# Spreading attention bias rows two heads at a time in a one-core encoder step

## The chip, the cores and the metric

The kernel runs on one core of one Trainium2 chip. A core has five engines with their own instruction queues, each served in order: TensorE (PE in the profile, with its weight loads listed apart as PEld) multiplies, VectorE (DVE) and ScalarE (ACT) work element by element and read the accumulators in PSUM, GpSimd (POOL) works on SBUF, and SyncE (SP) issues most of the transfers. Transfers are issued from the queues of SP, ACT and POOL, and the profile shows 16 DMA engines that carry them. The metric is the device time of one execution of the whole program in microseconds (us); lower is better.

## The reference

One layer of a streaming encoder runs for two groups of requests that share the weights: 2048 prompt rows and 128 sample rows (8 requests of 16 rows), 1024 wide. In float32:

```python
h = rms_norm(x, norm_g[0])
z = h @ w_in                      # q, k, v of attention (8 heads x 64); q, k, v, o of the mLSTM (4 x 128); gates
att = chunk-band attention(z)     # own 64-row chunk + 8 before it; + rel_bias(rel_table), clipped at 256
att = rms_norm(att, g_att)
hb  = mlstm_sequence(z)           # matrix memory with input and forget gates, running-max stabiliser
mix = concat(att, normed hb * sigmoid(o)) @ w_out
x   = x + rms_norm(mix, norm_g[1])
x   = x + rms_norm(conv_ffn(rms_norm(x, norm_g[2])), norm_g[3])
```

The sample rows attend to a cache of 512 keys and values per request and head and to their own 16 rows, and start the mLSTM from a given state. The outputs are the rows, the new keys and values, the memory's state and the convolution's tail. The bias of a score depends on the distance of query and key alone, so one row of 767 numbers per head holds all of it.

## The kernel before

All matrix products of the projections and of the feed-forward part are done in three passes: each operand is split into a high part (a cast to fp32r) and a low part (the difference), and `mm3` (L105 to L107) adds high x high, high x low and low x high in PSUM.

The program has two phases. In the first, the normed rows are transposed and multiplied by `w_in` in 14 groups of columns for each half of the rows (`GROUPS`: `va0`, `qk0`, `qk1`, `va1`, and so on to `vo3`). `group_T` and `group_rows` compute a group: each output tile is accumulated in one of two PSUM buffers (`ps_mm`), copied by ScalarE to one of two SBUF buffers (`st`), and stored to DRAM through ScalarE's queue (`qTd`, `kTd`, `vd`, `qkbd`, `vobd`). Group `va0` also holds the 8 gate columns, which go from PSUM to `gates` (L286). The weights of the next group are loaded and split during this one (`load_group`, L1228, L1234, L1235).

Beside a group, two pipes advance: attention and the mLSTM. A pipe is a list of units written as generators; `Pipe.step` takes a new unit and moves all live units one `yield` on, and `pump` steps the two pipes in turn as long as the work that they have asked of VectorE lags behind what the matrix products have asked of TensorE. `FLUSH` makes a pipe wait until its live units are done.

The attention pipe begins with `build_bias`: the reversed table is written to `ext` (one row of 767 per head, in DRAM), and for each head `ext`'s row is spread over 128 rows of `relrow` by one transfer (L317), so that a later load with a row step of 766 gives the bias of 128 queries. Two small transfers from GpSimd's queue (L322) then write a large number over two corners of each head's block, from the tile `outside`. `outside` is one of the three `raw` buffers that also take the raw queries, keys and values of each head. All 8 heads are done there, in one unit of 13 steps, ahead of the first head.

Then come the heads, by pairs, each with two groups `kg` of 512 rows in the first half (0 and 1) and two in the second (2 and 3): (0, kg 0), (1, kg 0), (0, kg 1), (1, kg 1), (2, kg 0) ... `load_head` issues on SP the load of the bias rows `nb` (L344, if `kg` is even), of the queries `qraw` (L351) and of the keys `kraw` (L354), casts them (L359, L363), and loads and casts the values; `att_unit` does scores, softmax and output. `attention_sample` handles the cached keys and values, request by request: `scores` loads the keys (L858) and multiplies (L874), `weights` does the softmax, `values` loads the cached values (L901) and multiplies (L915). Keys and values of a request take turns in the two buffers of `kh` and the two of `kl`. Each request's three units are followed by three empty ones.

In the last group, `w_out_steps` loads the eight row blocks of `w_out` and splits each in two column halves (L956 to L961): blocks 0 to 5 are loaded one by one, blocks 6 and 7 in one early load. `project` uses, for its first 512 output columns, all eight blocks' first halves. From row tile 8 on the second phase's work is mixed in; the second phase is the feed-forward part.

The order of instructions on each queue is not the order written: a planner with its own estimates of durations orders the program, earlier lines first among those that it takes to be ready, and allots buffers. An instruction under `keep_in_program_order` stays behind the instruction of its engine that was written just before it.

Of the kernel before, what the change touches and what calls it, by code (L numbers as in the profile page):

```python
# [17 lines left out]
P = 128  # L18
D = 1024
# [4 lines left out]
HA = 8  # L24
# [9 lines left out]
SQ = 127 + 640  # L34
# [16 lines left out]
def hymba_step(ctx: ExitStack, tc: tile.TileContext, I: dict, O: dict):  # L51
# [21 lines left out]
    def dt_(shape, name):  # L73
        return dram.tile(shape, F32, tag=name, name=name)
# [70 lines left out]
    def gate_ix(t):  # L145
        return 0 if t == SAMPLE else t + 1
# [124 lines left out]
    def group_rows(wh, wl, half, chunks, dst, name, width=256, out=None):  # L271
        for ci, tiles in enumerate(HALVES[half]):
            for j, t in enumerate(tiles):
                ch = chunks[ci]
                acc = ps_mm(f"{name}_{t}")
                for k in range(KT):
                    w = slice(k * width, (k + 1) * width)
                    tt = slice(j * P, (j + 1) * P)
                    mm3(acc[:, :width], ch[:, 0, k, tt], ch[:, 1, k, tt], wh[:, w], wl[:, w],
                        start=(k == 0), stop=(k == KT - 1))  # L280
                    if k % 4 == 3:
                        yield 1.3, 0.0
                stage = pa.tile([P, 384], F32, tag="st", name=f"{name}_st{t}", bufs=2)
                evac_scaled(stage[:, :256], acc[:, :256], None)
                if width > 256:
                    nc.vector.tensor_copy(gates[:, gate_ix(t), :], acc[:, 256:width])  # L286
                s = 4 if t == SAMPLE else t // 4
                nc.scalar.dma_start(dst[s][:, 0 if s == 4 else t % 4, :], stage[:, :256])
                if out is not None and s >= 3:
                    nc.scalar.dma_start(out[s - 3][:, 0 if s == 4 else t % 4, :], stage[:, :256])  # L290


    relrow = dt_([HA, P, SQ], "relrow")

    def raw_tile(name):
        return pa.tile([P, LS], F32, tag="raw", name=name, bufs=3)
# [3 lines left out]
    def load_bias():  # L300
        rel.append(raw_tile("reln")[:HA, :SQ - 383])
        tc.keep_in_program_order(nc.sync.dma_start(rel[0], I["rel_rev"][:, 0:SQ - 383]))

    def build_bias():
        ext = dt_([HA, SQ], "ext")

        def unit():
            far, near = raw_tile("relf")[:HA, :383], rel[0]
            nc.vector.tensor_scalar(near, near, -1.0, None, op0=ALU.mult)
            nc.vector.tensor_copy(far, near[:, 0:1].broadcast_to([HA, 383]))  # L310
            nc.sync.dma_start(ext[:, 383:SQ], near)
            nc.sync.dma_start(ext[:, 0:383], far)
            yield 0.0, 0.75
            big = raw_tile("outside")[:, :64]
            nc.vector.memset(big, BIG)
            for h in range(HA):
                tc.keep_in_program_order(nc.sync.dma_start(relrow[h], ext[h:h + 1, :].broadcast_to([P, SQ])))  # L317
                yield 0.0, 0.0
                for r, c in ((0, 576), (64, 0)):
                    at = bias_src(h, P, 640)  # L320
                    at = bass.AP(at.tensor, at.offset + r * (SQ - 1) + c, [[SQ - 1, 64], [1, 64]])
                    nc.gpsimd.dma_start(at, big[r:r + 64])  # L322
                if h % 2:
                    yield 0.0, 0.0

        yield unit()
        yield FLUSH
# [11 lines left out]

    def load_head(s):  # L340
        pair, kg, hh, h, nm = s.pair, s.kg, s.hh, s.h, s.nm
        if kg % 2 == 0:
            nb = pa.tile([P, 640], F32, tag="nb", name=f"nb{nm}", bufs=2)
            nc.sync.dma_start(nb, bias_src(h, P, 640))  # L344
            nbs[hh] = nb
        s.nb = nbs[hh]
        rows = slice(hh * 64, hh * 64 + 64)
        qr = raw_tile(f"qraw{nm}")[:, :512]
        krs = [raw_tile(f"kraw{nm}_{g}")[:, :512] for g in s.segs]
        for r in range(2):  # L350
            nc.sync.dma_start(qr[r * 64:r * 64 + 64, :], qTd[pair][kg][rows, :])  # L351
        for kr, g in zip(krs, s.segs):
            for r in range(2):
                nc.sync.dma_start(kr[r * 64:r * 64 + 64, :], kTd[pair][g][rows, :])  # L354
        yield 0.0, 0.0
        s.kh = pa.tile([P, 1024], F32R, tag="kh", name=f"kh{nm}", bufs=2)
        s.kl = pa.tile([P, 1024], F32R, tag="kl", name=f"kl{nm}", bufs=2)
        s.qs = pa.tile([P, 512], F32R, tag="qs", name=f"qs{nm}", bufs=2)
        nc.scalar.copy(s.qs, qr)  # L359
        nc.vector.tensor_tensor(s.qs[64:128], qr[64:128], s.qs[64:128], op=ALU.subtract)  # L360
        for si, kr in enumerate(krs):
            c = slice(si * 512, (si + 1) * 512)
            nc.scalar.copy(s.kh[:, c], kr)  # L363
            nc.vector.tensor_tensor(s.kl[:, c], kr, s.kh[:, c], op=ALU.subtract)
        new = [g for g in s.segs if g == kg or (h, g) not in vhl]
        vrs = [raw_tile(f"vraw{nm}_{g}")[:, :4 * DA].rearrange("p (a d) -> p a d", a=4) for g in new]
        for vr, g in zip(vrs, new):
            nc.sync.dma_start(vr, vd[h // 4][g][:, :, (h % 4) * DA:(h % 4 + 1) * DA])
        yield 0.0, 0.6 + 0.6 * len(krs)
        for vr, g in zip(vrs, new):  # L370
            t = pa.tile([P, 4, P], F32R, tag="vhl", name=f"vhl{nm}_{g}", bufs=4)
            nc.scalar.copy(t[:, :, 0:DA], vr)
            nc.vector.tensor_tensor(t[:, :, DA:P], vr, t[:, :, 0:DA], op=ALU.subtract)
            vhl[h, g] = t
        s.v = {g: vhl[h, g] for g in s.segs}
        if kg % 2:
            for g in s.segs:
                vhl.pop((h, g))
        yield 0.0, 0.34 * len(new)
# [456 lines left out]
    def attention_sample(b0, b1):  # L836
# [15 lines left out]
        def halves(name):  # L852
            return [pa.tile([P, 1024], F32, tag=tag, name=f"{name}{tag}", bufs=2) for tag in ("kh", "kl")]

        def scores(b):
            ks = halves(f"sk{b}")
            for i in range(2):
                nc.sync.dma_start(ks[i].rearrange("p (a k) -> p a k", a=2),  # L858
                                  I["cache_k"][b, 2 * i:2 * i + 2].rearrange("a p k -> p a k"))
            if b % 4 == 0 or b == b0:  # L860
                nc.sync.dma_start(own, kTs[:, :, b // 4 * 64:b // 4 * 64 + 64])
            yield 0.0, 0.0
            z = zs[b % 2].rearrange("p (a c) -> p a c", a=4)
            for hh in range(2):
                rr = slice(hh * 64, hh * 64 + 64)
                nc.vector.tensor_copy(z[rr, :, hh * DS:(hh + 1) * DS], qf[rr, :, b * DS:(b + 1) * DS])
            yield 0.0, 0.4
            yield 0.0, 0.0
            s.sp = ps_big(f"ss{b}")
            for o, n in ((0, 512), (512, DS)):  # L870
                for j in range(4):
                    k = ks[j // 2][:, j % 2 * 512:j % 2 * 512 + 512] if o == 0 else own[:, j, b % 4 * DS:b % 4 * DS + DS]
                    tc.keep_in_program_order(
                        nc.tensor.matmul(s.sp[32 * j:32 * j + 32, o:o + n], z[:, j, :], k, start=True, stop=True))  # L874
            yield 1.2, 0.0
# [21 lines left out]
        def values(b):  # L897
# [4 lines left out]
            tail = raw_tile(f"svt{b}")[:DS, :512]  # L902
            nc.sync.dma_start(tail, vs[b * DS:(b + 1) * DS, :])
            yield 0.0, 0.0
            yield 0.0, 0.0
            yield 0.0, 0.0
            yield 0.0, 0.0
# [25 lines left out]
    wo = []  # L933
# [3 lines left out]
    def w_out_steps():  # L937
# [5 lines left out]
        for k in range(KT):  # L943
            if k < 6:
                raw = pr.tile([P, 1056], F32, tag="wraw", name=f"wor{k}")[:, :D]
                nc.sync.dma_start(raw, I["w_out"][:, k * D:(k + 1) * D])
                if k == 0:
                    yield 0.0, 0.0
            else:
                raw = late[:, (k - 6) * D:(k - 5) * D]  # L950
            if k % 3 == 0:
                big.append(phT.tile([P, 6, D], F32R, tag="hT", name=f"wo{k}", bufs=3))
            h_, l_ = big[-1][:, k % 3 * 2, :], big[-1][:, k % 3 * 2 + 1, :]
            for c in (slice(0, 512), slice(512, D)):
                if k < 4:
                    nc.scalar.activation(h_[:, c], raw[:, c], AF.Copy, scale=gatt[:, k:k + 1])  # L956
                    nc.vector.scalar_tensor_tensor(l_[:, c], raw[:, c], gatt[:, k:k + 1], h_[:, c],
                                                   op0=ALU.mult, op1=ALU.subtract)
                else:
                    nc.scalar.copy(h_[:, c], raw[:, c])  # L960
                    nc.vector.tensor_tensor(l_[:, c], raw[:, c], h_[:, c], op=ALU.subtract)  # L961
                if k < 6:
                    yield 0.0, 0.6
            wo.append((h_, l_))

    def drain():
        while any([p_.step() for p_ in pipes]):
# [1028 lines left out]
```

## Time and profile before

| | us |
|---|---|
| median of 3 runs | 2762.39 |
| lowest and highest run | 2756.32, 2764.40 |
| profiled execution, its own time | 2761.56 |
| profiled execution, span | 2759.8 |
| TensorE busy in the span | 2659.9 |
| VectorE, ScalarE, GpSimd busy | 1862.4, 1417.6, 700.7 |

The span runs from the first to the last instruction that the profiler recorded; 1.8 us of the execution's own time lie around it. A view of waits adds up, for each group of instructions, the idle time of its engine just before it, and names what ended that idle time. A view of windows gives the busy time of each engine in a stretch, the clock that was granted to TensorE there (1.00 is full speed), and the DMA engines' mean busy share. In a timeline "SPq", "ACTq" and "POOLq" mark the issue of a transfer, and the bracket behind a row the idle time ahead of it.

### The profile page before, as it was taken

The page shows a single profiled execution, that of the slowest core. Times are in us where ns is not written, and L with a number is a line of the kernel's source. Part 1 is how long each engine was busy: PE and PEld are TensorE (multiplying, and loading weights), DVE is VectorE, ACT ScalarE, POOL GpSimd, SP SyncE. Part 2 cuts the span into 40 slices and gives each one's busy share as a digit, 9 for nine tenths or more (in the row PEclk, how much of TensorE's full clock was granted, in tenths as well). Part 3 has the DMA queues.
Part 4 walks back from the last instruction along what each step waited for, and adds up shares of the span by engine and source line. Part 5 has one row for each costly group of instructions (what it writes and reads, how often), then busy time and mean ns, then how long its engine had stood idle before and what let it go on. Part 6 is the DMA issues. An engine that isn't in the chain of part 4 may idle for free.

```text
span 2759.8 us, 47655 instructions
## 1 busy us (share of the span) xinstructions
PE 2659.9 (96%) x16459; PEld 2481.2 (90%) x16459; DVE 1862.4 (67%) x3536; ACT 1417.6 (51%) x2887; POOL 700.7 (25%) x1325
## 2 busy tenths in 40 slices
PE   8899999999999999979899999999999999999998
PEld 7899999999799998867799998889999878999976
DVE  5345445644355666556898998758888776899956
ACT  4345544533355665433454456655454665555554
POOL 1100000211000002344655542023333212466401
PEclk9999999999999999989999999999999999999999
DMA  5634454556743554469877768766786777788775
GB/s 173 171 114 138 122 186 140 172 176 196 225 135 116 157 178 146 146 228 308 298 246 215 214 198 265 251 208 195 223 219 192 228 252 238 213 246 237 253 257 183
DMA packets 333711, 555.70 MB, mean 201 GB/s; under 512 B 61762, under 2 KB 169374, under 8 KB 333150
## 3 DMA queue, kind: packets, MB, share of 16 engines
q1 hardware_dynamic: 250798, 405.03, 47.5%
q0 software_dynamic: 44080, 113.81, 14.1%
q10 hardware_dynamic: 38592, 33.83, 3.7%
q8 instruction: 129, 2.11, 0.3%
q14 instruction: 112, 0.92, 0.1%
HBM read 389.77 MB, written 172.18 MB: 204 GB/s over the span
## 4 chain that ended last, share of the span: by engine, by line
PE 41%; DMA 5%; DVE 4%; issue 2%; ACT 1%; POOL 0%; DVEq 0%; SPq 0%; POOLq 0%; ACTq 0%
PE uec L105 5%; PE uec L106 5%; PE uec L107 5%; PE dn L107 3%; PE dn L105 3%; PE dn L106 3%; PE ua L107 3%; PE ua L106 3%; PE ua L105 3%; DMA wu<-in_w_up 2%; PE dnm L107 1%; PE dnm L106 1%; PE dnm L105 1%; PE ub L107 1%; PE ub L106 1%
## 5 line engine op out<-in xcount | busy, mean ns | idle before, releaser
L105 PE MATMUL uec<-B,wuh 128*128 128x384 f32 (+1 forms) x720 | 236.6, 329 | 9.2 <-DVE ug L1495 5.9
L106 PE MATMUL uec<-B,wuh 128*128 128x384 f32 (+1 forms) x720 | 235.4, 327 | 0.0
L107 PE MATMUL uec<-B,wul 128*128 128x384 f32 (+1 forms) x720 | 234.3, 327 | 0.0
L1324 ACT CAST wuh<-wu 128x512 fp32r<-128x512 f32 x255 | 141.6, 618 | 102.6 <-PE uec L106 98.7
L107 PE MATMUL dn<-wdh,al 128*128 128x512 f32 x462 | 186.0, 403 | 3.4 <-DVE al L1325 3.4
L105 PE MATMUL dn<-wdh,ah 128*128 128x512 f32 x462 | 183.6, 397 | 5.9 <-ACT ah L1324 4.0
L1325 DVE TENSOR_TENSOR al<-ar,ah 128x768 fp32r<-128x768 f32 (+2 forms) x141 | 108.4, 779 | 118.4 <-ACT ah L1324 114.8
L106 PE MATMUL dn<-wdl,ah 128*128 128x512 f32 x462 | 182.8, 396 | 0.0
L1324 ACT CAST ah<-ar 128x768 fp32r<-128x768 f32 (+2 forms) x141 | 96.2, 692 | 153.2 <-PE dnm L106 113.9
L1325 DVE TENSOR_TENSOR wul<-wu,wuh 128x512 fp32r<-128x512 f32 x255 | 164.3, 682 | 2.4 <-ACT wuh L1324 2.4
L663 POOL TENSOR_SCALAR ad<-ad 128x2 f32<-128x2 f32 x32 | 6.3, 195 | 615.3 <-DVE ad L661 615.3
L410 DVE CUSTOM_DVE_ANT_0 tmp<-s,nb 128x640 f32<-128x640 f32 (+4 forms) x128 | 94.1, 737 | 100.1 <-PE s L400 99.5
L105 PE MATMUL vo<-wi_h,hT 128*128 128x256 f32 x544 | 155.5, 286 | 0.0
L107 PE MATMUL vo<-wi_h,hT 128*128 128x256 f32 x544 | 155.3, 285 | 0.0
L106 PE MATMUL vo<-wi_l,hT 128*128 128x256 f32 x544 | 154.9, 285 | 0.0
L1325 DVE TENSOR_TENSOR wdl<-wdr,wdh 128x512 fp32r<-128x512 f32 x231 | 145.3, 684 | 8.2 <-ACT wdh L1324 8.0
L105 PEld LDWEIGHTS uec<-B,wuh 128*128 128x128 f32 x720 | 135.2, 188 | 13.6 <-issue 6.8
L105 PE MATMUL qk<-hT,wi_h 128*128 128x384 f32 (+1 forms) x384 | 130.3, 339 | 9.9 <-ACT qk_st L239 6.2
L411 ACT ACTIVATE tmp<-tmp,mn 128x640 f32<-128x640 f32 (+4 forms) x128 | 97.7, 763 | 77.0 <-DVE mn L410 72.6
L106 PEld LDWEIGHTS uec<-B,wuh 128*128 128x128 f32 x720 | 135.4, 188 | 0.2
L107 PEld LDWEIGHTS uec<-B,wul 128*128 128x128 f32 x720 | 135.1, 188 | 0.0
L1324 ACT CAST wdh<-wdr 128x512 fp32r<-128x512 f32 x231 | 127.4, 619 | 11.8 <-PE uec L106 7.4
(473 smaller groups left out, 9101.8 us busy)
## 6 DMA issues: line engine op xcount, KB each, us to landing
wu<-in_w_up SPq DMA_DIRECT2D x220, 256.0 KB, 4.8
wu<-wsd SPq DMA_DIRECT2D x176, 256.0 KB, 4.7
wdr<-wtd SPq DMA_DIRECT2D x132, 256.0 KB, 5.1
wi_raw<-in_w_in SPq DMA_DIRECT2D x52, 512.0 KB, 4.2
wdr<-in_w_down SPq DMA_DIRECT2D x99, 256.0 KB, 4.7
wsd<-ws POOLq DMA_DIRECT2D x88, 256.0 KB, 4.8
ar<-ad_S SPq DMA_DIRECT2D x50, 384.0 KB, 4.0
kraw<-kTd SPq DMA_DIRECT2D x112, 128.0 KB, 3.1
```

Source lines behind the costliest of these rows:

```text
L105: nc.tensor.matmul(out, ah, bh, start=start, stop=False, skip_group_check=onto)
L106: nc.tensor.matmul(out, ah, bl, start=False, stop=False, skip_group_check=onto)
L107: nc.tensor.matmul(out, al, bh, start=False, stop=stop, skip_group_check=onto)
L410: nc.vector.tensor_tensor_reduce(o_, s_, b_, 1.0, 3e38, ALU.add, ALU.min, accum_out=mn)
L411: nc.scalar.activation(tmp[:, :n], tmp[:, :n], AF.Exp, bias=mn, scale=-1.0, accum_out=rsum[:, i % 4, hh:hh + 1])
L663: nc.gpsimd.tensor_scalar(ad, ad, 1.0 / DH, 0.0, op0=ALU.mult, op1=ALU.add)
L1324: nc.scalar.copy(h, r)
L1325: nc.vector.tensor_tensor(l, r, h, op=ALU.subtract)
```

## The change

Four edits:

1. **Bias rows.** `relrow` becomes one DRAM tile per head. `build_bias` spreads heads 0 and 1 alone. The spread of head h + 2, and its two corner writes, are issued at the head of `load_head` of head h with `kg` 1, ahead of that head's own loads. The corners' large number is first written to a DRAM tile, `corner`, and the corner writes read it from there, so the `raw` buffer `outside` is read by one transfer. The unit has 3 steps, where it had 13.
2. **Gates.** The 8 gate columns are copied out of PSUM by ScalarE, where VectorE copied them.
3. **Sample's keys.** The load of the next request's keys is written in the third step of `values`; it was written in the next request's `scores`, two steps on.
4. **Last rows of w_out.** Blocks 6 and 7 are split in the order 6 first half, 7 first half, 6 second half, 7 second half; it was 6 first, 6 second, 7 first, 7 second.

```diff
                 if width > 256:
-                    nc.vector.tensor_copy(gates[:, gate_ix(t), :], acc[:, 256:width])
+                    nc.scalar.copy(gates[:, gate_ix(t), :], acc[:, 256:width])
...
-    relrow = dt_([HA, P, SQ], "relrow")
+    relrow = [dt_([P, SQ], f"relrow{h}") for h in range(HA)]
+    ext = dt_([HA, SQ], "ext")
+    corner = dt_([P, 64], "corner")
...
+    def bias_rows(h):
+        tc.keep_in_program_order(nc.sync.dma_start(relrow[h], ext[h:h + 1, :].broadcast_to([P, SQ])))
+        for r, c in ((0, 576), (64, 0)):
+            at = bias_src(h, P, 640)
+            at = bass.AP(at.tensor, at.offset + r * (SQ - 1) + c, [[SQ - 1, 64], [1, 64]])
+            nc.gpsimd.dma_start(at, corner[r:r + 64])
+
     def build_bias():
-        ext = dt_([HA, SQ], "ext")
-
...
             nc.vector.memset(big, BIG)
-            for h in range(HA):
-                tc.keep_in_program_order(nc.sync.dma_start(relrow[h], ext[h:h + 1, :].broadcast_to([P, SQ])))
-                yield 0.0, 0.0
-                for r, c in ((0, 576), (64, 0)):
-                    at = bias_src(h, P, 640)
-                    at = bass.AP(at.tensor, at.offset + r * (SQ - 1) + c, [[SQ - 1, 64], [1, 64]])
-                    nc.gpsimd.dma_start(at, big[r:r + 64])
-                if h % 2:
-                    yield 0.0, 0.0
+            nc.sync.dma_start(corner, big)
+            for h in range(2):
+                bias_rows(h)
+            yield 0.0, 0.0
+            yield 0.0, 0.0
...
         pair, kg, hh, h, nm = s.pair, s.kg, s.hh, s.h, s.nm
+        if kg == 1 and h < HA - 2:
+            bias_rows(h + 2)
...
-        def scores(b):
-            ks = halves(f"sk{b}")
+        keys = {}
+
+        def fetch(b):
+            keys[b] = ks = halves(f"sk{b}")
             for i in range(2):
                 nc.sync.dma_start(ks[i].rearrange("p (a k) -> p a k", a=2),
                                   I["cache_k"][b, 2 * i:2 * i + 2].rearrange("a p k -> p a k"))
             if b % 4 == 0 or b == b0:
                 nc.sync.dma_start(own, kTs[:, :, b // 4 * 64:b // 4 * 64 + 64])
+
+        def scores(b):
+            if b not in keys:
+                fetch(b)
+            ks = keys.pop(b)
             yield 0.0, 0.0
...
             nc.sync.dma_start(tail, vs[b * DS:(b + 1) * DS, :])
             yield 0.0, 0.0
+            if b + 1 < b1:
+                fetch(b + 1)
             yield 0.0, 0.0
...
-            h_, l_ = big[-1][:, k % 3 * 2, :], big[-1][:, k % 3 * 2 + 1, :]
-            for c in (slice(0, 512), slice(512, D)):
+            wo.append((big[-1][:, k % 3 * 2, :], big[-1][:, k % 3 * 2 + 1, :]))
+
+            def cast(k, raw, c):
+                h_, l_ = wo[k]
...
+            for c in (slice(0, 512), slice(512, D)):
                 if k < 6:
+                    cast(k, raw, c)
                     yield 0.0, 0.6
-            wo.append((h_, l_))
+                elif k == 7:
+                    cast(6, late[:, :D], c)
+                    cast(7, late[:, D:], c)
```

## The prediction, made before the changed kernel ran

> **What bounds the kernel now.** I read the engines' totals first, then TensorE's waits, then the granted clock around the longest of them, then the timelines of the engines that ended them.
>
> ```profile
> span 2759.8 us, 47655 instructions
> PE 2659.9 (96%) x16459; PEld 2481.2 (90%) x16459; DVE 1862.4 (67%) x3536; ACT 1417.6 (51%) x2887; POOL 700.7 (25%) x1325
> ```
>
> TensorE is busy in all but about 100 us, and the change removes none of its instructions. It can gain only where TensorE idles. All edits lie in the first phase or at its end; these are the waits there that they touch (in us: total, times, longest).
>
> ```profile
> PE qk L105 <- ACT qk_st L239: 6.2, 1, 6.2
> PE ss L874 <- DMA sk6kh<-in_cache_k: 3.2, 1, 3.2
> PE qk L105 <- ACT qk_st L237: 3.1, 1, 3.1
> PE va L105 <- DVE gates L286: 2.3, 1, 2.3
> PE wo L106 <- DVE wo L961: 1.4, 1, 1.4
> PE rt L77 <- DVE cm L571: 1.2, 1, 1.2
> ```
>
> Behind a wait the clock can fall as well. In the view of windows (stretch, its length, busy time of PE, PEld, DVE, ACT, POOL, then the granted clock, the DMA share and GB/s) these stretches follow the waits of 3.1, 6.2, 2.3 and 3.2 us:
>
> ```profile
> 84.00:90.00 6.00, 5.75 (x18) 5.30 (x19) 2.70 (x8) 1.72 (x4) 0.00 (x0) 0.50 0.49 163
> 111.00:114.00 3.00, 3.00 (x10) 3.00 (x10) 0.33 (x1) 0.48 (x1) 0.85 (x3) 0.50 0.80 217
> 536.00:541.00 5.00, 4.60 (x25) 4.61 (x26) 3.82 (x12) 2.23 (x8) 2.02 (x5) 0.66 0.62 190
> 714.00:718.00 4.00, 4.00 (x19) 2.35 (x19) 0.00 (x0) 0.48 (x1) 0.23 (x2) 0.59 0.74 232
> ```
>
> Busy time at a clock below 1.00 is partly lost: 5.75 x 0.50 = 2.9 us, 3.00 x 0.50 = 1.5, 4.60 x 0.34 = 1.6 and 4.00 x 0.41 = 1.6. A removed wait returns both parts. [...]
>
> **Bias rows: the first stall.** Timeline rows of SP, DVE and ACT, the landing times of `relrow`'s transfers (least, median, most), and the median landing of `qraw` and `kraw` in the whole run:
>
> ```profile
> 58.80 4.09 SPq L317 DMA_DIRECT2D relrow<-ext  x4
> 66.58 2.82 SPq L317 DMA_DIRECT2D relrow<-ext  x2
> 78.71 0.41 DVE L571 TENSOR_TENSOR_SCAN cm<-ap 32x128 f32<-32x128 f32 x1 [4.83 <-DMA mds<-cms]
> 83.20 0.62 ACT L359 CAST qs<-qraw 128x512 fp32r<-128x512 f32 x1 [11.31 <-DMA qraw<-qTd]
> DMA to landing us min/median/max: 1.8/6.8/9.5
> qraw<-qTd SPq DMA_DIRECT2D x64, 128.0 KB, 3.5
> kraw<-kTd SPq DMA_DIRECT2D x112, 128.0 KB, 3.1
> ```
>
> Six of the eight spreads are issued within 11 us. While they move, ScalarE idles 11.3 us for the first head's queries, and right behind the cast L359 comes the copy L237 that ended TensorE's wait of 3.1 us in the list above. The 1.2 us for `cm` are the same crowding: the scan waited for a 2 KB store to land. With six spreads gone from here, the queries should land in 3.5 us, where the spreads themselves take 6.8 in the median: 3.3 us sooner, an estimate, and more than 3.1. I take 3.1 + 1.2 + 2.9 = **7.2 us**, with 4.3 (the clock falls all the same) and 7.2 as bounds.
>
> **The second stall.**
>
> ```profile
> 101.05 1.16 SPq L317 DMA_DIRECT2D relrow<-ext  x2
> 102.25 1.23 SPq L354 DMA_DIRECT2D kraw<-kTd  x2
> 104.90 0.39 ACT L706 ACTIVATE w<-mb,colsp 128x128 f32<-128x128 f32 x1
> 109.57 0.62 ACT L363 CAST kh<-kraw 128x512 fp32r<-128x512 f32 x1 [4.29 <-DMA kraw<-kTd]
> 110.10 0.48 ACT L239 ACTIVATE qk_st<-qk 128x384 f32<-128x384 f32 x1
> ```
>
> The last two spreads are issued right ahead of head 1's keys, and ScalarE waits for those keys with TensorE's copy L239 behind. Without the spreads the keys are issued at 101.1 and land 3.1 later, at 104.2. What is late next is ScalarE itself: L706 ends at 105.3, the cast takes 0.53 until the copy starts, the copy 0.48, so TensorE goes on at 106.4 where it went on at 110.6. Its gap shrinks from 6.2 to 2.0: 4.2 us. Whether 2.0 us still bring the clock down, the rows leave open (2.3 did), so I take half of 1.5. Together 4.2 + 0.75 = **4.95 us**; bounds 0 (ScalarE's order has another wait next) and 7.7 (the gap goes altogether). [...]
>
> **Where the six spreads go.** Each now stands ahead of the loads of a head with `kg` 1, costs SP about 0.6 us of issue (1.16 for two), and delays the loads behind it. Behind two spreads the keys issued at 102.25 were cast at 109.57, where 3.1 of landing would have made it 105.4: 4 us for two, so one costs 2, and 2.6 us with its issue. The tightest of these heads, head 1:
>
> ```profile
> 131.56 5.19 SPq L354 DMA_DIRECT2D kraw<-kTd  x4
> 143.49 1.14 ACT L363 CAST kh<-kraw 128x512 fp32r<-128x512 f32 x2 [0.56 <-PE s L399]
> 108.25 1.08 POOL L322 DMA_DIRECT2D relrow<-outside  x2 [4.76 <-DMA relrow<-ext]
> 150.00:350.00 200.00, 200.00 (x1406) 198.99 (x1405) 95.44 (x203) 101.88 (x229) 0.00 (x0) 1.00 0.42 125
> ```
>
> The last keys are issued by 136.8 and, at 3.1, landed at 139.9; the cast comes at 143.5, and TensorE's scores ended its wait, not the transfer. 3.6 us cover 2.6: cost 0. Uncovered, ScalarE would stand up to 2.6 us per head, 16 us for six; that is the worst case, and it needs the cover gone six times. GpSimd stands while a spread lands (4.8 us in the third row) with its masks and powers behind it. Between 150 and 350 us it has nothing else to do (its column in the fourth row is 0), so the four spreads that fall there hold nobody. The spread of heads 0 and 1 is the exception, since it may now begin much sooner:
>
> ```profile
> 11.49 0.30 SPq L311 DMA_DIRECT2D ext<-reln  x1
> 19.99 0.19 POOL L88 TENSOR_SCALAR n_ms<-ssq 128x1 f32<-128x1 f32 x1 [5.09 <-ACT hT L229]
> ```
>
> It is pinned behind the `corner` store, which needs one memset and no weights. `ext` is written from 11.5 us on, so the spread can stand between the first row tiles' norms, and GpSimd's `n_ms`, on the way to TensorE's transposes, behind its corner writes. Most it costs: a hold of 4.8 plus a clock stretch of 2.9, 7.7 us. I take 0, as GpSimd idles about 5 us between two norms. The `raw` buffer that `outside` frees helps the first heads' loads, at no price I can read.
>
> **Gates.** For the wait at 536 the view names VectorE; the timeline shows that ScalarE was late:
>
> ```profile
> 535.78 0.36 ACT L237 COPY va_st<-va 128x256 f32<-128x256 f32 x1
> 536.17 0.17 DVE L286 COPY gates<-va 128x8 f32<-128x8 f32 x1
> L530 ACT ACTIVATE lg_e_s<-lg_e_s 128x4 f32<-128x4 f32 x1 | 0.2, 215 | 0.0
> ```
>
> The gates follow ScalarE's own copy of the tile within 0.03 us. Moved behind it on ScalarE, they end at 536.14 + 0.2 = 536.35, as before. 17 copies cost ScalarE 17 x 0.215 = 3.7 us, beside TensorE, and spare VectorE 2.7. Sum **0**; bounds 3.9 gained (2.3 and its 1.6 of clock, were the order better) and 0.7 lost.
>
> **Keys.** The rows behind the wait of 3.2 us:
>
> ```profile
> 705.17 0.42 SPq L901 DMA_DIRECT2D sv5kl<-in_cache_v  x1
> 705.63 0.43 SPq L858 DMA_DIRECT2D sk6kh<-in_cache_k  x1
> SPq L681 <- DMA md<-cm: 4.9, 1, 4.9
> ```
>
> The keys are issued straight behind the values of the request before; the planner had already drawn them forward. What made both late is SP standing 4.9 us for `md`, an mLSTM load, which stays. The program places the new fetch behind these values as well. I take **0**; bounds 4.8 gained (3.2 + 1.6) and the loss in the fourth rival.
>
> **w_out.**
>
> ```profile
> 1023.55 1.67 ACT L960 CAST wo<-wor 128x512 fp32r<-128x512 f32 x3
> 1026.56 1.14 ACT L960 CAST wo<-wor 128x512 fp32r<-128x512 f32 x2
> 1029.56 0.23 DVE L509 TENSOR_SCALAR hgm<-hgm 128x128 f32<-128x128 f32 x1 [1.73 <-DMA hgm<-in_g_mlstm]
> ```
>
> Blocks 6 and 7, loaded early, are the casts that end at 1025.2. The pair at 1026.6 is block 4, whose difference came late because VectorE stood for `hgm`. Swapping two of the four changes nothing that TensorE waits for: **0**, at best the 1.4 us.
>
> **Sum.** 7.2 + 4.95 = 12.15 us against the profiled execution's own time of 2761.56 (span 2759.8 and 1.8 around it), 0.8 below the median of 2762.39: 2761.56 - 12.15 = **2749.4 us**. The second phase has no absolute start, so it moves forward whole.
>
> **Rivals.**
>
> 1. *The keys come free too.* If the new order puts their fetch ahead of `md`, 4.8 us go, and with the rest of the second stall's clock 0.75: 2749.4 - 5.55 = 2743.9. For it: transfers stand ready far ahead of use elsewhere. Against: the buffers pass from values to keys in turn, so the values go first.
> 2. *The relief is half.* The second stall stays, as ScalarE in its fixed order finds another late load (L706 had just waited for a mask): 2761.6 - 7.2 = 2754.4. Or the second goes too, and the early spread holds the norms: 2749.4 + 7.7 = 2757.1. Middle 2755.7: no change that can be told.
> 3. *It does not do what it says.* The planner draws the six free spreads forward again into the crowded 60 to 110 us. Each is pinned behind the SP instruction written before it, which speaks against. Then 2761.6.
> 4. *Slower: the sooner keys hold SP.*
>
> ```profile
> SPq L858 <- PE ss L874: 8.5, 1, 8.5
> ```
>
> This is the key load of request 1, on SP, waiting 8.5 us for TensorE to leave the buffer, with the weights of the next group and the heads' loads behind it. It cost nothing there. A fetch two steps sooner meets that buffer sooner, for requests 3 to 7 beside other loads that TensorE needs. At the price of the one wait of this place, 4.8 each, five cost 24: 2749.4 + 24 = 2773. From the third on (14.4) it outweighs the gain, from the fifth the result is measurably slower.
>
> **How the numbers follow.** Forecast 0.47, rival 1 0.13, rival 2 0.18, rival 3 0.09, rival 4 0.13. A difference of 0.3% (8.3 us) is about what can be told from none. The forecast and rival 1 are faster by more: 0.60. Rivals 2 and 3 are within: 0.27. Rival 4 is slower: 0.13. Lower end of the range: all upper bounds at once but the gap's rest, 12.15 + 0.75 + 4.8 + 3.9 + 1.4 = 23, hence 2738. Upper end: first stall alone with the early hold, 2761.6 - 7.2 + 7.7 = 2762, and 2 us for one key fetch half paid, 2764. That leaves out most of rival 4. Forecast and rival 1 alone: 2738 to 2754.
>
> **What would show it.** Right: no run of six L317 rows between 58 and 70 us; L359 and L363 of the first two heads landing in 3 to 4 us; TensorE's waits for `qk_st` down from 9.3 to about 2 us, and the clock at 1.00 from 84 to 90. Wrong: waits on `qk_st` as long, under another releaser; a new TensorE wait on `xr` before 50 us; key loads on SP waiting for `ss` with weights late behind them. The gates' and w_out's waits should stay, or go for reasons of order alone.

## The result and the profile after

The changed kernel takes 2749.18 us (median of five executions, 2746.58 to 2750.97), the kernel before beside it 2759.64: ratio **0.9961, interval 0.9945 to 0.9977**. That is 6 to 15 us faster. The forecast was 2749.4. Its profiled execution took 2750.46 us, span 2748.7. Of the executions in the experiments below, one of bias_wout (5260.41 us) and one of late_and_keys (11993.73 us) took far longer than the rest: the medians count them, the ratios do not.

The number was right, but the profile shows that it was not made up of the terms that I had summed. First the waits of TensorE in the changed kernel (us: total, times, longest):

```profile
PE spt L77 <- ACT stmp L897: 6.2, 2, 4.0
...
PE cus L803 <- DMA cs<-in_state_c: 4.0, 4, 2.1
...
PE pt L77 <- ACT tmp L416: 3.6, 3, 3.1
...
PE s L404 <- DVE ptl L428: 3.2, 2, 2.9
...
PE va L105 <- ACT gates L286: 2.0, 1, 2.0
...
PE ss L886 <- DMA sk4kh<-in_cache_k: 0.3, 1, 0.3
```

No wait for `qk_st` is left (9.3 us before) and the wait for the sample's keys fell from 3.2 to 0.3. In their place stand waits that the kernel before did not have, or had shorter: `stmp`, `cs`, `tmp`, `ptl`.

Timeline rows of the changed kernel (SP's issues, ScalarE's casts), in order of time:

```profile
16.02 1.21 SPq L307 DMA_DIRECT2D relrow<-ext  x2
...
67.62 1.13 SPq L356 DMA_DIRECT2D qraw<-qTd  x2
...
70.77 0.62 ACT L364 CAST qs<-qraw 128x512 fp32r<-128x512 f32 x1 [0.55 <-DMA qraw<-qTd]
...
90.67 1.09 SPq L359 DMA_DIRECT2D kraw<-kTd  x2
...
99.30 0.62 ACT L368 CAST kh<-kraw 128x512 fp32r<-128x512 f32 x1 [3.33 <-DMA kraw<-kTd]
100.03 0.51 SPq L307 DMA_DIRECT2D relrow<-ext  x1
```

The spreads are where the prediction put them: two at 16 us, the others one by one between 100 and 256 us (three of them before 130). ScalarE waits 0.55 us for the first head's queries, before 11.31. It still waits 3.33 us for the second pair of keys (4.29 before).

Next the windows view of TensorE by stage: stretch, its length, busy time of PE, granted clock, DMA share, GB/s. The kernel before:

```profile
14.00:60.00 46.00, 43.12 (x321) 1.00 0.40 127
60.00:130.00 70.00, 59.52 (x342) 0.90 0.65 175
330.00:745.00 415.00, 404.98 (x3235) 0.99 0.59 183
1060.00:1200.00 140.00, 133.37 (x749) 0.99 0.46 147
1200.00:1330.00 130.00, 109.78 (x484) 0.91 0.86 290
1330.00:1440.00 110.00, 106.00 (x594) 1.00 0.79 267
```

and the changed kernel:

```profile
14.00:60.00 46.00, 39.88 (x299) 1.00 0.46 148
60.00:130.00 70.00, 65.18 (x394) 0.98 0.59 151
330.00:745.00 415.00, 396.31 (x3144) 0.99 0.58 177
1060.00:1200.00 140.00, 129.94 (x715) 0.99 0.49 158
1200.00:1330.00 130.00, 121.92 (x573) 0.97 0.94 331
1330.00:1440.00 110.00, 105.87 (x601) 1.00 0.76 240
```

Length less busy time is what TensorE idles; busy time at a clock below 1.00 counts as lost for the missing share. "Lost" below is the sum of both (the clock at its steps in the trace, finer than these two digits):

| lost by TensorE, us | before | after | difference | forecast |
|---|---|---|---|---|
| 14 to 60 (start-up) | 2.9 | 6.1 | +3.2 | 0 |
| 60 to 130 (both stalls) | 15.1 | 6.5 | -8.6 | -12.15 |
| 330 to 745 (heads, samples) | 13.4 | 22.1 | +8.7 | 0 |
| 745 to 1060 | 10.8 | 7.3 | -3.5 | 0 |
| 1060 to 1440 (output projection, first FFN blocks: "the project stage") | 41.9 | 27.1 | -14.8 | 0 |
| of it 1200 to 1330 | 29.6 | 11.2 | -18.4 | 0 |
| 1440 to the end (9 us of it behind TensorE's last instruction, in both) | 32.1 | 30.4 | -1.8 | 0 |

The rows down to the end add up to -16.8, and the span fell by 11.1. The clock's share is an upper estimate: over the whole span it fell by 10.8, and the busy time of TensorE, with as many instructions, by only 5.7 (2659.9 to 2654.2); with 5.5 us less of idle time that makes the 11.1. The largest term, -18.4 in 1200 to 1330 us (12.1 of it idle time), lies in a stage that no edit touches.

### The profile page after: what moved, and what is told of

Same layout as the page of the kernel before. It is cut to its first block, busy times and chain, and to the rows that moved or that the text cites. A ratio compares the mean times of both kernels' runs of the same rounds, so it can differ in the third digit from the quotient of the medians.

```text
span 2748.7 us, 47667 instructions
## 1 busy us (share of the span) xinstructions
PE 2654.2 (97%) x16459; PEld 2476.4 (90%) x16459; DVE 1861.1 (68%) x3519; ACT 1418.8 (52%) x2904; POOL 694.6 (25%) x1325
## 3 DMA queue, kind: packets, MB, share of 16 engines
q0 software_dynamic: 44080, 113.81, 14.2%
## 4 chain that ended last, share of the span: by engine, by line
PE 42%; DVE 4%; DMA 4%; issue 1%; ACT 1%; POOL 0%; DVEq 0%; SPq 0%; POOLq 0%; ACTq 0%
PE uec L105 5%; PE uec L106 5%; PE uec L107 5%; PE dn L107 3%; PE dn L105 3%; PE dn L106 3%; PE ua L107 3%; PE ua L105 3%; PE ua L106 3%; PE ub L107 1%; PE ub L106 1%; PE ub L105 1%; PE dnm L107 1%; PE dnm L106 1%; PE dnm L105 1%
## 5 line engine op out<-in xcount | busy, mean ns | idle before, releaser
L415 DVE CUSTOM_DVE_ANT_0 tmp<-s,nb 128x640 f32<-128x640 f32 (+4 forms) x128 | 94.3, 737 | 91.8 <-PE s L405 91.1
L428 DVE TENSOR_TENSOR ptl<-pt,pth 128x640 fp32r<-128x640 f32 (+4 forms) x128 | 93.5, 738 | 56.8 <-ACT pth L427 56.1
```

Of the source, the lines that this page charges most:

```text
L415: nc.vector.tensor_tensor_reduce(o_, s_, b_, 1.0, 3e38, ALU.add, ALU.min, accum_out=mn)
L428: nc.vector.tensor_tensor(s.ptl[:, sl, qc], ptv, s.pth[:, sl, qc], op=ALU.subtract)
```

## The experiments

Theory **R**: the gain is the relief of 60 to 130 us, and the rest is chance. Theories beside it: **P**, any edit draws another order; **S**, the bias edit also takes ten empty steps out of the attention's pipe, which starts sooner, and everything behind moves. All results first; the columns by stage are us lost by TensorE, and the last one says when SP issued the last store of the mLSTM. Times are compared by the ratio to the kernel before on the same chip, with its 95% interval; executions of one kernel differ by up to some 20 us, so a stage's figure from its one profile is read only where several kernels agree. The profiled execution need not be a typical one either: that of bias_only (2731.50 us) was its fastest, that of after_padded (2764.79) lay 6 us above its median.

| kernel | ratio | 14-60 | 60-130 | 330-745 | 1060-1440 | last `mixd<-num`, us |
|---|---|---|---|---|---|---|
| before | 1 | 2.9 | 15.1 | 13.4 | 41.9 | 1208.8 |
| all four edits | 0.9961 (0.9945-0.9977) | 6.1 | 6.5 | 22.1 | 27.1 | 1190.2 |
| rest_only | 1.0000 (0.9989-1.0011) | 2.1 | 16.3 | 14.2 | 39.9 | 1211.6 |
| bias_only | 0.9936 (0.9917-0.9954) | 5.6 | 3.5 | 16.0 | 28.8 | 1180.2 |
| fewer_steps | 0.9997 (0.9984-1.0009) | 2.0 | 12.6 | 18.7 | 30.9 | 1199.8 |
| after_padded | 1.0001 (0.9988-1.0015) | 9.0 | 8.1 | 16.5 | 44.4 | 1213.3 |
| bias_gates | 0.9954 (0.9937-0.9971) | 8.7 | 4.9 | 21.6 | 29.1 | 1187.7 |
| bias_keys | 0.9924 (0.9906-0.9942) | 8.6 | 5.3 | 20.4 | 28.6 | 1188.0 |
| bias_wout | 0.9941 (0.9923-0.9959) | 5.7 | 5.2 | 18.8 | 26.4 | 1182.6 |
| late_corners | 0.9915 (0.9897-0.9932) | 3.0 | 5.0 | 19.9 | 28.2 | 1181.8 |
| folds_on_sp | 1.0011 (0.9998-1.0024) | 2.7 | 14.6 | 12.4 | 47.1 | 1205.9 |
| all_but_gates | 0.9946 (0.9931-0.9960) | 6.0 | 5.2 | 22.7 | 26.9 | 1186.5 |
| late_and_keys | 0.9937 (0.9924-0.9951) | 2.9 | 4.9 | 20.8 | 29.7 | 1184.8 |
| fewer_bubbles | 0.9978 (0.9962-0.9994) | 2.6 | 15.1 | 13.7 | 43.4 | 1211.4 |

**Which edit: bias_only and rest_only.** The kernel before with the bias edit alone, and with the three other edits alone.

> The kernel before with the bias edit alone. Theory R (relief): what was gained is the bias edit's, from the six spreads that no longer crowd 58 to 115 us, so nearly all of it appears: 2749 to 2752 us, TensorE's lost time between 60 and 130 us (idle plus clock) down from 15.1 to about 6.5, the waits for qk_st gone. Theory P (new order): the larger part came from the project stage at 1200 to 1330 us, which no edit touches and which the planner ordered anew; then that part appears with some edits and not with others: 60 to 130 gains its 8 us again, but start-up (0 to 60) gives back 3, and without a gain at 1200 to 1330 (29.6 us lost there, 11.2 with all edits) the time is 2756 or more.

> The kernel before with the gates, the sooner keys and the w_out split, and with the old bias rows. Theory R: no gain, 2756 to 2763 us, 15.1 us lost between 60 and 130 as before. Theory P: the stage at 1200 to 1330 us is drawn anew by these edits too, so the time can move by up to 18 us although nothing at 60 to 130 changed; if it is below 2752, the bias edit isn't what counts.

2737.32 and 2756.92 us. The three small edits together are worth nothing (within 0.11%), as forecast. The bias edit is worth 0.46 to 0.83%, 13 to 23 us, more than the 12.15 us summed for it. By the middle value it is also worth more than the four together, though the two intervals overlap a little (0.9945 to 0.9954). Its relief of 60 to 130 us is 11.6 in this profile (15.1 to 3.5), so R holds for that stage, but not for the whole: R's time was 2749 to 2752. 1060 to 1440 gained another 13.1, and in rest_only, whose order also differs, it did not. P in its plain form falls: it isn't any new order that helps.

**The two halves of the bias edit: fewer_steps and after_padded.**

```diff
 # fewer_steps, on the kernel before
             for h in range(HA):
                 tc.keep_in_program_order(nc.sync.dma_start(relrow[h], ...))
-                yield 0.0, 0.0
 ...
-                if h % 2:
+                if h % 4 == 3:
                     yield 0.0, 0.0
 # after_padded, on the changed kernel
             for h in range(2):
                 bias_rows(h)
-            yield 0.0, 0.0
-            yield 0.0, 0.0
+            for _ in range(12):
+                yield 0.0, 0.0
```

> The kernel before with ten of the thirteen empty steps of its bias build taken out; all eight spreads stay, one behind the other. The attention's pipe starts ten steps sooner, as in the changed kernel, but the spreads still stand together. Theory R: the crowd stays a crowd, the lost time at 60 to 130 stays above 12 us and the whole at 2756 to 2764 us. Theory S (the earlier start of the attention is what moves everything behind it): 2750 to 2753 us, with the project stage at 1200 to 1330 losing about 11 us in place of 29.6.

> The changed kernel with ten empty steps put back behind the first two spreads, so that the attention's pipe starts as late as before the change, with the six other spreads still with their heads. Theory R: 2747 to 2752 us, lost time at 60 to 130 about 6.5 us. Theory S: the sooner start is gone, the project stage loses 25 us or more again, and the time is 2758 us or more.

2755.68 and 2758.44 us. By stages each half does much of what S and R say, though S's time for fewer_steps (2750 to 2753) and R's for after_padded (2747 to 2752) were both missed: without the ten steps 1060 to 1440 loses 30.9 us although the eight spreads stand in one run at 57.9 us; with the steps put back it loses 44.4 although the spreads are spread out, and 60 to 130 still keeps its relief (8.1). By these profiles the project stage belongs to the sooner start, and the relief to the spreads. By the time neither half alone gains anything that can be told. For after_padded the stages say why: the early spread costs 6.1 us at start-up, clock included, the pipes are late again, and 7.0 us of relief are eaten. For fewer_steps they don't: its profiled execution was its fastest, 2749.35 us against a median of 2755.68, so its row is better than the kernel. That the two together give 17.6 us where each gives none within 5 is measured; why they multiply rather than add stays open. after_padded also carries the cost of the early spread, so what the relief is worth alone, without that cost, was not measured.

What the sooner start moves is seen in the SP timeline at the end of the mLSTM. The kernel before:

```profile
1208.80 0.37 SPq L672 DMA_DIRECT2D mixd<-num  x1
...
1209.76 2.64 SPq L1083 DMA_DIRECT2D x2r<-x2d  x4
```

and bias_only:

```profile
1180.23 0.37 SPq L677 DMA_DIRECT2D mixd<-num  x1
...
1183.42 1.64 SPq L1088 DMA_DIRECT2D x2r<-x2d  x2
...
1213.15 0.94 SPq L1088 DMA_DIRECT2D x2r<-x2d  x2
```

`open_ffn` takes over the memory of the first phase, so the FFN's first rows `x2r` are loaded within 5 us behind the last store of the mLSTM, in every kernel here. The last column of the table parts the kernels in two: where that store was issued at 1180 to 1200 us, 1060 to 1440 loses 26 to 31 us (nine kernels); where at 1206 to 1213, 40 to 47 (five).

**What holds the project stage: folds_on_sp.** In the kernel before, TensorE's longest wait there, 6.0 us for `x2r`, ends at 1224 us. GpSimd's timeline just ahead of it:

```profile
1219.84 0.55 POOL L1181 DMA_DIRECT2D fold<-in_w_down  x1 [5.37 <-DMA wtd<-fold]
...
1222.45 0.57 POOL L94 TENSOR_TENSOR n_rs<-n_ms,nhalf 128x1 f32<-128x1 f32 x1
```

The norm's power stands behind a load of the w_down fold that waited 5.4 us for a store to land. In this kernel the fold's loads and stores are SP's:

```diff
-                keep(nc.gpsimd.dma_start(live[k, x], I["w_down"][k][:, x * 512:(x + 1) * 512]))
+                keep(nc.sync.dma_start(live[k, x], I["w_down"][k][:, x * 512:(x + 1) * 512]))
 ...
-                keep(nc.gpsimd.dma_start(wtd[k][:, x * 512:(x + 1) * 512], live.pop((k, x))))
+                keep(nc.sync.dma_start(wtd[k][:, x * 512:(x + 1) * 512], live.pop((k, x))))
```

> The kernel before, with the loads and stores of the w_down folds (L1181, L1188) issued by SP in place of GpSimd; nothing else. Theory Q (in the kernel before GpSimd's queue is what holds the project stage: a fold load stands 5.4 us for a store to land, the powers of the norms behind it come late, TensorE waits 6.0 us for x2r at 1218 us): that wait goes, the lost time at 1200 to 1330 falls from 29.6 to 12 to 18 us, and the time to 2745 to 2752 us. Theory L (the stage is held by late work ahead of it, or by DVE's own wait for fold, 19.2 us in seven): the lost time stays above 22 us and the time within 5 us of 2760. SP may take up the waits for the stores itself, with the loads of x2r and of the weights behind it; then the time rises.

2757.76 us, and 40.8 us lost at 1200 to 1330: Q falls in this form. L's figures were met, but for the reason in the last sentence: SP took up the waits. The time did not rise by anything that can be told (0.9998 to 1.0024). First GpSimd's wait in the kernel before (1180 to 1330 us), then the waits in this kernel:

```profile
POOL fold L1181 <- DMA wtd<-fold: 16.9, 9, 5.4
...
SPq L1181 <- DMA wtd<-fold: 16.9, 16, 4.1
...
PE h2T_pt L1111 <- DVE x2r L1103: 28.8, 4, 19.3
```

The 16.9 us of standing for the fold's stores now sit on SP, with the loads of `x2r` behind them.

**Another way to end the pipes sooner: fewer_bubbles.**

```diff
         yield own()
-        for _ in range(3):
+        for _ in range(1):
             yield bubble()
```

> The kernel before, with one empty step in place of three behind the first unit of each of the four sample heads of the mLSTM (eight steps less in the memory pipe); bias rows, attention and everything else as before. In every kernel so far the first loads of x2r stand on SP right behind the last mLSTM store mixd<-num; where that store was issued at 1206 to 1213 us, four x2r loads stood in one run and 1200 to 1330 lost 28 us or more; where it was at 1180 to 1200 us, two and two, 11 to 15 us. Theory S (what decides the project stage is how soon the pipes end, whatever makes them end): the two-and-two order with the store some 5 us sooner is enough, 1200 to 1330 loses 12 to 20 us, TensorE's wait for x2r shrinks from 7.5 to below 3 us, and the time is 2745 to 2756 us. Theory B (it needs the bias edit's or the attention's earlier start itself): 25 us or more lost there, 2757 to 2765 us.

2752.51 us, a ratio of 0.9978. TensorE's wait for `x2r` is all but gone, with the same view of the kernel before behind it (each from 1180 to 1330 us):

```profile
PE h2T_pt L1111 <- DVE x2r L1103: 1.4, 1, 1.4
```

```profile
PE h2T_pt L1111 <- DVE x2r L1103: 7.5, 2, 6.0
```

The stretch of 1200 to 1330 loses 18.0 us, inside S's figures. But the last mLSTM store did not come sooner (1211.4), and 1060 to 1440 as a whole lost 43.4: what went at 1200 came back before 1200 (+6.4) and behind 1330 (+6.6). So the figures that I had set for S were met without its cause. The wait for `x2r` does not make up what the stage costs: removing it did not shorten the stage. The kernel is faster by a little all the same (0.9962 to 0.9994, 2 to 10 us); in this one profile what went lies behind 1440 us (22.6 lost, 32.1 before), and why stays open. What the sooner end frees in those 11 to 15 us is not pinned to one wait here.

**The small edits beside the bias edit: bias_gates, bias_keys, bias_wout, all_but_gates.**

> The bias edit and the gates on ScalarE; keys and w_out as before. The bias edit alone gave 2737.3 us, all four edits 2749.2, so the three small edits cost about 12 us beside it, though alone they cost nothing (2756.9 against 2758.2). Theory G (the gates are the cost: ScalarE, with the copy in front of L416 and L897, holds TensorE): 2746 us or more, and the wait pt L77 <- ACT tmp at 98 us (3.1 us, 1.5 with the bias edit alone) stays. Theory O (each small edit draws another order, and what they cost is the sum of chance waits): 2740 to 2745 us, with the added waits at other places than in the changed kernel.

> The bias edit and the sooner keys; gates and w_out as before. Theory K (the sooner keys are the cost: the sample's steps at 690 to 745 us lost 9.6 us with all edits, 3.7 with the bias edit alone, behind the wait spt L77 <- ACT stmp): 2744 us or more, with that wait at 6 us again. Theory O: 2737 to 2743 us, the wait near the 2.6 us that it has with the bias edit alone.

> The bias edit and the split of the last w_out rows; gates and keys as before. The order differs only behind 1000 us. Theory W (the split is the cost, by what it moves in the projection): 2744 us or more, with the extra loss between 1000 and 1700 us. Theory O: 2735 to 2741 us; the lost time up to 1000 us as with the bias edit alone.

> The changed kernel with the gates back on VectorE. Ratios to the kernel before so far: all four edits 0.9961, bias 0.9936, bias and gates 0.9954, bias and keys 0.9924, bias and w_out 0.9941. Theory G (the gates on ScalarE cost some 5 to 9 us): 0.992 to 0.994, so 2738 to 2744 us. Theory O (the sum of chance in the order): anywhere between 0.992 and 0.997, with no relation to the gates; a value of 0.9955 or more would clear the gates.

2746.24, 2737.24, 2743.42 and 2742.26 us. Theory K falls: with the keys 0.9924, no worse than the bias edit alone, though the wait `spt <- stmp` stood at 4.6 us. Theory W isn't supported: 0.9941, a time between the two forecasts. For the gates both pairs have the same sign, 0.9954 against 0.9936 and 0.9961 against 0.9946, each about 4 to 5 us slower with the gates on ScalarE; but the intervals overlap, so a cost of the gates is likely and not shown. The place that theory G named is not it: TensorE's wait for `tmp` near 98 us is 2.5 with the gates on ScalarE (bias_gates) and 3.1 with the gates back on VectorE (all_but_gates).

**The start-up hold: late_corners and late_and_keys.** In bias_only, GpSimd's timeline:

```profile
23.93 0.73 POOL L311 DMA_DIRECT2D relrow<-corner  x1 [8.44 <-DMA relrow<-ext]
24.74 0.18 POOL L88 TENSOR_SCALAR n_ms<-ssq 128x1 f32<-128x1 f32 x1
24.98 1.54 POOL L311 DMA_DIRECT2D relrow<-corner  x3
26.54 1.09 POOL L94 TENSOR_TENSOR n_rs<-n_ms,nhalf 128x1 f32<-128x1 f32 x1
```

The corner writes of heads 0 and 1 are then queued behind the last norm of the first half (`powers` collects the norms' power instructions):

```diff
+            with tc.issue_after(powers[-1].ins) if h < 2 else nullcontext():
                 nc.gpsimd.dma_start(at, corner[r:r + 64])
 ...
     def load_head(s):
+        if kg == 0 and h < 2:
+            corners(h)
```

> The bias edit alone, with the corner writes of heads 0 and 1 queued on GpSimd behind the last norm of the first half (n_16) in place of between the norms. With the bias edit alone GpSimd stands 8.4 us at 24 us for the first two spreads, and TensorE then waits 2.4 us for xr; the stretch of 14 to 60 us loses 5.6 us, before 2.9. If that hold is the cost, it is gone: 2 to 3 us lost at 14 to 60, no wait of TensorE for xr behind 20 us, and 2733 to 2736 us. If the norms were late for another reason (their rows land late, ScalarE), 14 to 60 stays at 5 to 6 us and the time at 2736 to 2740. A loss behind it, 2740 or more, would come from the rows nb, which now wait for the corners until about 48 us with the weights wi_raw behind them on SP.

> The bias edit with the late corners of heads 0 and 1, and the sooner keys; gates and w_out as before. If the two gains add: late corners 0.9915 and the keys 0.9924 against 0.9936 for the bias edit alone make 0.990 to 0.991, 2732 to 2735 us. If they are chance of the order: 0.991 to 0.994.

2735.58 and 2738.75 us. GpSimd's timeline in late_corners:

```profile
19.82 0.19 POOL L88 TENSOR_SCALAR n_ms<-ssq 128x1 f32<-128x1 f32 x1 [4.85 <-ACT hT L231]
20.09 0.55 POOL L96 TENSOR_TENSOR n_rs<-n_ms,nhalf 128x1 f32<-128x1 f32 x1
...
44.51 2.24 POOL L318 DMA_DIRECT2D relrow<-corner  x4
```

The norm that came at 24.74 comes at 19.82, and 14 to 60 loses 3.0 and 2.9 us in the two kernels, as in the kernel before (2.9): the hold was the cost of start-up. By the time the 2.6 us can't be told (0.9915 and 0.9937 against 0.9936). late_corners is faster than the kernel before, and than the changed one too: its interval ends at 0.9932, where that of the changed kernel begins at 0.9945. The gains of late corners and keys didn't add: 0.9937.

## Why the prediction was right, and where it was wrong

- **The first stall, 7.2 us: right in mechanism.** No run of six spreads, queries cast 2.0 us behind the end of their issue, no wait for `qk_st`. From 60 to 95 us TensorE lost 7.2 us before and loses 0.5 now, so 6.7 came. The windows view of the changed kernel (PE, PEld, DVE, ACT, POOL, granted clock, DMA share, GB/s) has the clock at 1.00 where it was 0.50:

```profile
84.00:90.00 6.00, 6.00 (x35) 5.74 (x34) 2.00 (x7) 2.14 (x4) 0.00 (x0) 1.00 0.43 112
```

- **The second stall, 4.95 us: right in kind, too large.** From 95 to 130 us the loss fell from 7.9 to 6.0, so 1.9 came (2.6 to 4.5 in the seven other kernels that hold the bias edit without padding). I left 2.0 us of wait and half of the clock's 1.5. What stands there now is 3.1 us for `tmp` at 98 us, and 3.41 us at a clock of 0.50, from 102.8 us: the second pair of keys, issued by 91.8, was cast at 99.3, 7.5 us later, where I had written 3.1. A weight load of 512 KB (`wi_raw`) was issued just ahead of these keys, at 89.4; that it held them is not shown. With both stalls the stage gained 8.6 of the forecast 12.15; over the eight kernels that hold the bias edit without padding 8.6 to 11.6, about 10.
- **The early spread, taken at 0: the wrong step.** I argued from 5 us of idle between two norms and a hold of 4.8. GpSimd stood 8.0 us for the two spreads (8.4 in bias_only's row above), with a norm behind it. It cost 3.2 us here, and 5.7 to 6.1 in bias_gates, bias_keys and after_padded; in the last the clock fell too, to 0.93 from 14 to 60 us. My bound of 7.7 held, my value didn't. What I gave as the upper end, the first stall gained alone and the norms held (2762), is near to what after_padded shows: 2758.44, with 7.5 us still lost from 95 to 130.
- **The six moved spreads at 0: right.** 130 to 330 us loses at most 1.2 us in any of the kernels.
- **Gates, keys, w_out at 0: right as a sum** (rest_only). The keys' wait did go, which I had given to rival 1, but not by the keys edit: it is 0.8 us in bias_only, which lacks that edit, and 2.9 and 1.8 for two requests in rest_only, which has it. In the same steps a wait `spt <- stmp` of 6.2 us stands now (2.6 in bias_only). Rival 4 didn't come: SP's key loads wait 10.5 us for `ss`, 8.3 of it in one wait (8.5 before).
- **The step that is missing.** My sum has no term for the removed lines `yield 0.0, 0.0`, which issue no instruction. They are ten steps by which the attention's pipe runs ahead. Its first scores (`s`) begin hardly sooner, at 93.2 us in place of 95.7; its last begin at 1105.0 in place of 1121.5, and at 1126.1 in after_padded. In the changed kernel that goes with -14.8 us in a stage a thousand us later and with more lost between 330 and 745: 16.0 to 22.7 us in the nine kernels with ten steps less, 12.4 to 16.5 in the five others. "The second phase has no absolute start, so it moves forward whole" was wrong: what the first phase's end does to the project stage was the largest term of all.
- **So the total** of -10.8 us (-6 to -15) came near 12.15 because +3.2 and +8.7 that I had at zero met -14.8 and -3.5 that I had at zero too. That they met so closely was luck. The forecast faster was right for the reason given only in its first part, and that part alone did not make the kernel faster: after_padded keeps 7.0 us of the relief and has a ratio of 1.0001.

## What to carry to other kernels

An empty step in a pipelined schedule is an edit like any other: ask which pipe starts sooner by it, and read what stands behind that pipe's end, however far. A transfer that an engine's own queue waits for can hold what stands behind it on that engine (here a norm, behind GpSimd's hold of 8.0 us; in bias_only, with 8.4, it came at 24.74 us, in late_corners at 19.82); price it with that transfer's landing in its new place, not with its median elsewhere. And a stretch that loses less is no proof while its neighbours aren't counted: in fewer_bubbles 11.6 us vanished from one window and 13.0 came back beside it.

## What the runs showed of the hardware

In the profiles of the two kernels it did not go by the length of the idle time alone whether the clock fell: 1.85 us left it at 1.00, 1.71 did not. The windows view around the waits at 536 and 710 us (stretch, length, PE busy, clock, DMA share, GB/s; length less busy time is idle), the kernel before:

```profile
533.82:537.24 3.42, 1.10 (x10) 1.00 0.36 105
537.24:540.65 3.41, 3.41 (x18) 0.50 0.78 261
540.65:544.06 3.41, 3.41 (x32) 1.00 0.81 236
707.90:711.31 3.41, 2.13 (x13) 1.00 0.97 380
711.31:714.72 3.41, 1.42 (x6) 1.00 1.01 371
714.72:718.14 3.42, 3.42 (x17) 0.50 0.72 216
```

and the changed kernel:

```profile
532.89:536.30 3.41, 1.56 (x14) 1.00 0.31 60
536.30:539.72 3.42, 3.19 (x25) 1.00 0.99 322
...
724.03:727.44 3.41, 1.16 (x10) 1.00 1.02 298
727.45:730.86 3.41, 3.41 (x13) 0.50 1.10 264
```

The stretches with 2.3 and 2.0 us idle in the kernel before (to 537.24 and 714.72) and with 2.25 in the changed one (to 727.44) were followed by one at 0.50; those with 1.3 (to 711.31) and with 1.85 (to 536.30, in the changed kernel) were followed by one at 1.00. The 1.71 us idle from 1011.70 to 1015.11, in the kernel before, were followed by 0.50 too. What decides it is not shown. A stretch of 3.41 us at 0.50, busy throughout, counts as 3.41 x 0.50 = 1.7 us lost in the tables above; by the busy time of the two kernels (5.7 us less, where the clock's share fell by 10.8) I estimate that about half of that was lost. By the same count bias_gates lost 23.0 us to the clock, where bias_keys lost 16.2 with as much idle time (86.3 and 85.3); the mean clock of their profiled executions was 0.99 and 0.993.
